# First token tile's experts looked up in two halves of the heads, its row gathers begun during the key rounds, and the key compares fed from PSUM

## The chip, the cores and the metric

The program runs on 1 core of one Trainium2 chip, alone, as one launch. The metric is the device time of one execution in microseconds (us). The core has TensorE (PE; its weight loads are listed as PEld), VectorE (DVE), ScalarE (ACT), GpSimd (POOL), SyncE (SP, which here only issues transfers) and 16 DMA engines. Each engine runs its own instruction list in order.

## The reference, cut to what matters

The program computes two layers of a first block (feed-forward, three attentions, feed-forward), a recurrent mixer, and at the end a layer of 16,384 experts ("peer") and a last normalization. Only the peer layer is touched. For 512 tokens of width 1024:

```
qry    = (t @ w_q).reshape(n_tok, 8 heads, 2 sides, 128)
scores = einsum("thpd,hpkd->thpk", qry, sub_keys)              # 128 keys a side
s_top, i_top = top_k(scores, 16)
cand     = (s_top[:, :, 0, :, None] + s_top[:, :, 1, None, :])   # 16 x 16 pairs a head
cand_idx = (i_top[:, :, 0, :, None] * 128 + i_top[:, :, 1, None, :])
best, pos = top_k(cand, 16)
idx  = take_along_axis(cand_idx, pos);  gate = softmax(best)
act  = gelu(einsum("td,thkd->thk", t, u_tab[idx]))
out  = einsum("thk,thkd->td", gate * act, v_tab[idx])
```

So each token uses 8 x 16 = 128 of the 16,384 experts; an expert is one row of `u_tab` and one row of `v_tab`, 1024 numbers each.

## The kernel before

The peer layer works on four token tiles of 128 tokens. Tile 0 takes the rows of its own experts from HBM ("gathered"). Tiles 1 to 3 (384 tokens) do it densely: all 16,384 experts are computed for all 384 tokens, and a gate matrix that is zero nearly everywhere multiplies them. The layer has four stages.

**Key rounds** (`topk`, L1600 to L1624). Sixteen rounds j, two for a head. A round multiplies a weight column block by the hidden state, scores it against the keys (L1607), and VectorE takes the 16 best of each of four tiles (`top16`). At odd j GpSimd adds the candidate sums `cand` (L1618) and VectorE takes the best pairs of tiles 0 and 1 (`pair`). A weight block is loaded into `raw`, rounded by ScalarE into `wh` (L91), and the rest `wl` is subtracted (L92): in this stage by GpSimd. From j = 4 on each round also computes one dense group of 128 experts in advance (`ahead`, 53 of the 128 groups in all, list `EARLY`) and stores it to HBM.

**Lookup** (`found`). It turns positions of best pairs into key numbers and gates: a wide compare on VectorE (L1674), a product on GpSimd (L1675), a sum on VectorE (L1678), twice. For tile 0 it ends in `eidx` and `egate`. For tiles 1 to 3, TensorE turns the results into a PSUM bank `pt` (L1706) and ScalarE copies them to SBUF tiles `sel`. Before the change the lookups of tile 0 and tile 1 run together after the last key round, with five `ahead` groups beside them (L1658).

**Scatter** (`scatter`, L1712 to L1751). It builds the gate matrix of tiles 1 to 3 in 24 blocks of 16 tokens. For every token a one-hot `lt` (VectorE, L1728) and a weighted one-hot `rt` are made and multiplied on TensorE into `g`; `rt` is made partly by ScalarE (L1734, L1735), partly by a VectorE compare (L1737) and a GpSimd product (L1738). A block holds two half blocks of eight tokens. The other `ahead` groups run here, 36 in number, and so do the lookups of tiles 2 and 3.

**Dense stage** (`dense`, L1552 to L1577). 16 groups g of eight expert groups e; from e = 1 of the next group on, eight `down` blocks use the eight results. The gates `gt` of a group are loaded at e = 0, 1.5 MB in one transfer. The product is split as `eh` (ScalarE) and `el` (GpSimd, L1569).

**The gathered rows of tile 0** (`gathered`) are a generator of 256 rows of each token, four from `pur` then four from `pvr` in turn. One step (`more(1)`) issues the gather of one row on GpSimd (L1472, 512 KB) and uses an earlier one on VectorE: a dot product with `ht` (L1479) or a multiply-add into `acc` (L1486). LOOK says how many steps lie between a row's issue and its use. Four buffers `er` hold rows, so a gather waits until the row four before it is used. `more` is called at chosen places of the scatter and the dense stage; issues and uses keep their order among themselves, and a list scheduler puts them between the other instructions.

PSUM has three `bk` banks for linear products, two `sc`, two `g` and one `pt`.

Of the kernel before, what the change touches and what calls it, by code (L numbers as in the profile page):

```python
# [9 lines left out]
F = mybir.dt.float32  # L10
FR = mybir.dt.float32r
BF = mybir.dt.bfloat16
I32 = mybir.dt.int32
# [13 lines left out]
D = 1024  # L27
# [23 lines left out]
class K:  # L51
# [1403 lines left out]
    def gathered(self, ht):  # L1455
# [4 lines left out]
        NB, LOOK = 4, 2  # L1460
# [7 lines left out]
        for n in range(len(steps) + LOOK):  # L1468
            if n < len(steps):
                table, s = steps[n]  # L1470
                r = rows[n] = mp.tile([128, D], F, name="er", tag="er", bufs=LOOK + 2)
                order(nc.gpsimd.indirect_dma_start(r, None, a[table], bass.IndirectOffsetOnAxis(ap=self.eidx[:, s:s + 1], axis=0)))  # L1472
            if n >= LOOK:
                table, s = steps[n - LOOK]
                r, b, i = rows.pop(n - LOOK), s // NB, s % NB
                if table == "pur":
# [4 lines left out]
                    if i == NB - 1:  # L1481
                        w = ws[b] = mp.tile([128, NB], F, name="ew", bufs=3)
                        nc.scalar.activation(w, dots.pop(b), AF.Gelu)
                        nc.vector.tensor_mul(w, w, self.egate[:, NB * b:NB * b + NB])
# [4 lines left out]
    def peer(self):  # L1489
# [6 lines left out]
        with tc.tile_pool(name="peer", bufs=1) as mp:  # L1496
# [3 lines left out]
            sel = [mp.tile([128, DW], F, name=f"sel{i}") for i in range(4)]  # L1500
            ht = self.by_token(rc)
            self.eidx = mp.tile([128, 128], I32, name="eidx")
            self.egate = mp.tile([128, 128], F, name="egate")
# [23 lines left out]
    def dense(self, ep, mp, gd, ad, dn, expert, more):  # L1527
# [24 lines left out]
        for g in range(16):  # L1552
            wh, wl = [], []
            for e in range(8):
# [17 lines left out]
                more(0 if j in EARLY else 1 + (e == 0))  # L1572
# [6 lines left out]
    def topk(self, sp, hh, hl, io, sel, gd, ahead, more):  # L1579
# [13 lines left out]
        with tc.tile_pool(name="topk1", bufs=1) as mp:  # L1593
# [31 lines left out]
            first = mp.tile([128, 4, 8, 16], F, name="first")  # L1625
            nc.vector.tensor_copy(first, si[:, :, :, 0])
            nc.vector.tensor_copy(second, si[:, :, :, 1])

            sf = first.rearrange("p t h k -> p (t h) k")
            pk = mp.tile([128, 32, 16], F, name="pk")  # L1630
            rw = row.rearrange("p t h k -> p (t h) k")
            nc.vector.tensor_tensor(pk, sf, io[:, 160:176].unsqueeze(1).to_broadcast([128, 32, 16]), op=OP.add)
            nc.vector.tensor_copy(rw[:, :, 0:1], pk[:, :, 0:1])
            nc.vector.tensor_tensor(rw[:, :, 1:16], pk[:, :, 1:16], pk[:, :, 0:15], op=OP.subtract)
        with tc.tile_pool(name="topk2", bufs=1) as mp:
# [22 lines left out]
            run(pairs(0), pairs(1), fill(5, 0))  # L1658
# [3 lines left out]
    def found(self, mp, t, best, pos, second, row, io, sel):  # L1662

        nc = self.nc
        b3, b4 = [128, 8, 16], [128, 4, 16, 16]
# [5 lines left out]
        def look(dst, src, table, values, op):  # L1671
            for q in (slice(0, 4), slice(4, 8)):
# [12 lines left out]
        z = mp.tile([128, 8], F, name="gz", bufs=2)  # L1685
# [12 lines left out]
        if t * 128 < SPT:  # L1698
            nc.vector.scalar_tensor_tensor(res[0], res[0], 128.0, res[1], op0=OP.mult, op1=OP.add)
            nc.vector.tensor_copy(self.eidx, res[0].rearrange("p h k -> p (h k)"))  # L1700
# [6 lines left out]
        for i in range(3):  # L1707
            nc.scalar.copy(sel[i][:, s0:s0 + 128], pt[:, i * 128:i * 128 + 128])
# [215 lines left out]
```

## Time and profile before

| | us |
|---|---|
| median of 3 runs | 4782.38 (4781.05 to 4784.15) |
| profiled execution, its time | 4788.46 |
| its span | 4786.7 |
| key rounds, 16 of them | about 3316 to 3459 |
| from the last key scores to the first full scatter block | 3459 to 3516 |
| scatter | 3516 to 3840 |
| dense stage with its last products | 3840 to 4740 |
| end | 4740 to 4787 |

Over the span PE is busy 94%, DVE 66%, ACT 40% and POOL 26%. These shares say little, since the stages have different limits: the peer layer has to be read stage by stage, in the table of busy times by stretch, and in the list of who waited for whom in a stretch. All times below are counted from the start of the span.

### The profile page before, as it was taken

What the parts mean: (1) busy time and instruction counts of PE and PEld (TensorE: products, weight loads), DVE (VectorE), ACT (ScalarE), POOL (GpSimd) and SP (SyncE); (2) the same over time, 40 slices, a digit from 0 to 9 for tenths busy, and PEclk for the clock granted to TensorE, in tenths of its full rate; (3) what the DMA queues carried; (4) which work ended last, traced back from release to release, by engine and by line L of the source; (5) the groups of instructions that cost most, each with busy time, mean ns of one, the idle gap of its engine ahead of it and who ended that gap; (6) DMA issues with size and microseconds to landing.
All of it is one profiled execution on the core that took longest, in us unless ns stands there. A gap on an engine that the chain in (4) does not pass through costs nothing. (4 is left out here: it accounts for less than half of the span.)

```text
span 4786.7 us, 63161 instructions
## 1 busy us (share of the span) xinstructions
PE 4504.0 (94%) x23078; PEld 3895.2 (81%) x23078; DVE 3179.3 (66%) x5824; ACT 1919.9 (40%) x3465; POOL 1223.6 (26%) x1053
## 2 busy tenths in 40 slices
PE   9999998999999999989999998988968889999998
PEld 7887876788888888767788777876967889999998
DVE  4447878754454458787644467876598767777776
ACT  3225665632232246646422333223355633333333
POOL 0001112210000011121300101223577744555543
PEclk9999999999999999999999999998988999999999
DMA  3234323433323344233423334123346787788884
GB/s 128 95 105 131 98 83 93 151 113 97 97 93 97 97 126 112 87 98 98 158 96 97 122 90 141 45 65 119 119 168 217 256 270 272 272 282 284 296 279 171
DMA packets 282359, 696.58 MB, mean 146 GB/s; under 512 B 32864, under 2 KB 98304, under 8 KB 278976
## 3 DMA queue, kind: packets, MB, share of 16 engines
q1 hardware_dynamic: 245184, 558.30, 36.5%
q0 software_dynamic: 36864, 134.23, 8.0%
q8 instruction: 183, 3.00, 0.3%
q14 instruction: 128, 1.05, 0.1%
HBM read 597.18 MB, written 72.17 MB: 140 GB/s over the span
## 5 line engine op out<-in xcount | busy, mean ns | idle before, releaser
L91 ACT CAST wh<-raw 128x1024 fp32r<-128x1024 f32 (+3 forms) x773 | 765.9, 993 | 1669.1 <-PE bk L113 959.4
L113 PE MATMUL bk<-hh,wh 128*128 128x512 f32 (+1 forms) x3016 | 1140.3, 378 | 15.8 <-ACT hh L237 9.0
L113 PE MATMUL bk<-hh,wl 128*128 128x512 f32 (+1 forms) x3016 | 1133.8, 376 | 8.2 <-DVE wl L92 8.2
L113 PE MATMUL bk<-hl,wh 128*128 128x512 f32 (+1 forms) x3016 | 1133.2, 376 | 0.5 <-DVE hl L238 0.5
L92 DVE TENSOR_TENSOR wl<-raw,wh 128x1024 fp32r<-128x1024 f32 (+3 forms) x664 | 812.2, 1224 | 174.5 <-ACT wh L91 166.9
L113 PEld LDWEIGHTS bk<-hh,wh 128*128 128x128 f32 x3016 | 574.6, 191 | 97.0 <-ACT hh L237 9.4
L113 PEld LDWEIGHTS bk<-hh,wl 128*128 128x128 f32 x3016 | 573.9, 190 | 87.5 <-DVE wl L92 9.3
L113 PEld LDWEIGHTS bk<-hl,wh 128*128 128x128 f32 x3016 | 574.8, 191 | 79.1 <-issue 2.2
L203 POOL TENSOR_TENSOR sq<-sq,sqt 128x512 f32<-128x512 f32 x61 | 102.2, 1675 | 1199.7 <-ACT sqt L199 1180.9
L92 POOL TENSOR_TENSOR wl<-raw,wh 128x1024 fp32r<-128x1024 f32 (+2 forms) x109 | 258.3, 2371 | 583.3 <-ACT wh L91 463.7
L113 PE MATMUL bk<-eh,wl 128*128 128x384 f32 x1024 | 354.8, 346 | 41.7 <-DVE wl L92 41.4
L113 PE MATMUL bk<-eh,wh 128*128 128x384 f32 x1024 | 350.7, 342 | 2.5 <-ACT act L1513 1.8
L113 PE MATMUL bk<-el,wh 128*128 128x384 f32 x1024 | 350.1, 342 | 0.6 <-POOL el L1569 0.6
L113 PE MATMUL bk<-gh,wh 128*128 128x512 f32 x704 | 273.9, 389 | 0.0
L113 PE MATMUL bk<-gh,wl 128*128 128x512 f32 x704 | 273.9, 389 | 0.0
L113 PE MATMUL bk<-gl,wh 128*128 128x512 f32 x704 | 273.9, 389 | 0.0
L1569 POOL TENSOR_TENSOR el<-act,eh 128x384 fp32r<-128x384 f32 x128 | 176.4, 1382 | 336.5 <-ACT eh L1568 327.2
L276 DVE TENSOR_TENSOR t<-bk,rr 128x512 f32<-128x512 f32 x88 | 60.8, 691 | 269.1 <-PE bk L113 269.1
L113 PEld LDWEIGHTS bk<-eh,wl 128*128 128x128 f32 x1024 | 194.9, 190 | 53.4 <-DVE wl L92 53.4
L1486 DVE SCALAR_TENSOR_TENSOR acc<-er,ew,acc 128x1024 f32<-128x1024 f32 x128 | 179.7, 1404 | 80.3 <-DMA er<-in_pvr,eidx 80.3
L1479 DVE CUSTOM_DVE_ANT_0 er<-er,ht 128x1024 f32<-128x1024 f32 x128 | 172.8, 1351 | 77.9 <-DMA er<-in_pur,eidx 77.9
L285 DVE SCALAR_TENSOR_TENSOR x<-bk,x 128x512 f32<-128x512 f32 x96 | 66.4, 692 | 231.4 <-PE bk L113 231.4
(709 smaller groups left out, 8784.5 us busy)
## 6 DMA issues: line engine op xcount, KB each, us to landing
raw<-in_wi SPq DMA_DIRECT2D x176, 512.0 KB, 3.6
raw<-in_pu SPq DMA_DIRECT2D x128, 512.0 KB, 4.7
raw<-in_pv SPq DMA_DIRECT2D x128, 512.0 KB, 4.3
raw<-in_wo SPq DMA_DIRECT2D x64, 448.0 KB, 3.3
raw<-in_mg SPq DMA_DIRECT2D x48, 512.0 KB, 3.7
gate_d<-stage SPq DMA_DIRECT2D x24, 1024.0 KB, 7.0
gt<-gate_d SPq DMA_DIRECT2D x16, 1536.0 KB, 11.0
raw<-in_wo SPq DMA_DIRECT2D x32, 512.0 KB, 3.5
```

The lines of the kernel that those rows point to most:

```text
L91: self.nc.scalar.copy(wh[:, :n], raw[:, :n])
L92: (eng or self.nc.vector).tensor_sub(wl[:, :n], raw[:, :n], wh[:, :n].bitcast(F))
L113: self.nc.tensor.matmul(ps, x[:, c], y[k], start=(n == 0), stop=(n == 3 * kk - 1))
L203: nc.gpsimd.tensor_add(self.sq, self.sq, t)
L276: nc.vector.tensor_mul(t2, pb, rr)
L285: nc.vector.scalar_tensor_tensor(self.x[m], ps, 0.5, self.x[m], op0=OP.mult, op1=OP.add)
L1479: order(nc.vector.tensor_tensor_reduce(out=r, in0=r, in1=ht, scale=1.0, scalar=0.0, op0=OP.mult, op1=OP.add, accum_out=dots[b][:, i:i + 1]))
L1486: order(nc.vector.scalar_tensor_tensor(acc, r, ws[b][:, i:i + 1], acc, op0=OP.mult, op1=OP.add))
L1569: nc.gpsimd.tensor_sub(q, act, h.bitcast(F))
```

## The change

Four things are edited.

1. Tile 0's lookup runs in two halves of four heads, inside the key rounds, at the end of j = 7 and of j = 15; `eidx` and `egate` become two tiles of 64 columns. The preparation of `row` and `second` is halved with it.
2. Row steps of tile 0 start earlier: three in each of rounds 8 to 15, two with each of the five `ahead` groups after the last round. In return the dense stage has them only at e = 0, 1 and 7 and in the `down` blocks. Over all 34 steps come before the scatter (none before), 48 in it (48 before), and the dense stage has 176 (211 before). LOOK goes from 2 to 3, the buffers stay four.
3. The scatter's compares L1728 and L1737 read the selected keys from the PSUM bank (now an `sc` bank, one for each tile in turn) and not from SBUF; the copy of `sel[0]` goes.
4. In every second scatter block one `ahead` group's `wl` moves from GpSimd to VectorE, 12 in all.

```diff
-        NB, LOOK = 4, 2
+        NB, LOOK = 4, 3
...
-                r = rows[n] = mp.tile([128, D], F, name="er", tag="er", bufs=LOOK + 2)
-                order(nc.gpsimd.indirect_dma_start(r, None, a[table], bass.IndirectOffsetOnAxis(ap=self.eidx[:, s:s + 1], axis=0)))
+                r = rows[n] = mp.tile([128, D], F, name="er", tag="er", bufs=LOOK + 1)
+                order(nc.gpsimd.indirect_dma_start(r, None, a[table], bass.IndirectOffsetOnAxis(ap=self.eidx[s // 64][:, s % 64:s % 64 + 1], axis=0)))
...
-                more(0 if j in EARLY else 1 + (e == 0))
+                more((2 - g % 2 if e == 0 else 1) if e in (0, 1, 7) else 0)
...
+                if j % 8 == 7:
+                    hs = slice(j // 8 * 4, j // 8 * 4 + 4)
...
+                    for _ in self.found(mp, 0, best[:, 0, hs], pos[:, 0, hs], second[:, 0, hs], row[:, 0, hs], io, sel, j // 8):
+                        pass
+                if j >= 8:
+                    more(3)
...
-            run(pairs(0), pairs(1), fill(5, 0))
+            run(pairs(1), fill(5, 2))
...
-        pt = self.bank("pt")
+        pt = self.bank("sc")
...
-                nc.vector.tensor_tensor(lt, keys(8), wide(sel[0], 0, 8), op=OP.is_equal)
+                nc.vector.tensor_tensor(lt, keys(8), wide(pt, 0, 8, i - s0), op=OP.is_equal)
...
-                    nc.vector.tensor_tensor(r, keys(4 - n), wide(sel[1], u + n, u + 4), op=OP.is_equal)
-                    nc.gpsimd.tensor_tensor(r, r, wide(sel[2], u + n, u + 4), op=OP.mult)
+                    nc.vector.tensor_tensor(r, keys(4 - n), wide(pt, u + n, u + 4, i - s0 + 128), op=OP.is_equal)
+                    nc.gpsimd.tensor_tensor(r, r, wide(sel[1], u + n, u + 4, i), op=OP.mult)
...
-                    ahead(1, nc.gpsimd if tb % 2 else None)
+                    ahead(1)
```

The order of instructions on POOL changes at three places. First, POOL in the key rounds, from the candidate sums of round 11 to those of round 13 (`cand` are candidate sums, `wl` weight splits, `er` the gathers). Before:

```order
L1618 TENSOR_TENSOR cand<-sv 128x4x8
L92 TENSOR_TENSOR wl<-raw,wh 128x1024
L1618 TENSOR_TENSOR cand<-sv 128x4x16
L92 TENSOR_TENSOR wl<-raw,wh 128x1024 x3
L1618 TENSOR_TENSOR cand<-sv 128x4x8
```

After:

```order
L1619 TENSOR_TENSOR cand<-sv 128x4x8
L92 TENSOR_TENSOR wl<-raw,wh 128x1024
L1619 TENSOR_TENSOR cand<-sv 128x4x16
L1472 DMA er<-in_pvr,eidx_29050 128x1024 x2
L1472 DMA er<-in_pur,eidx_29050 128x1024
L92 TENSOR_TENSOR wl<-raw,wh 128x1024 x2
L1472 DMA er<-in_pur,eidx_29050 128x1024 x3
L92 TENSOR_TENSOR wl<-raw,wh 128x1024
L1619 TENSOR_TENSOR cand<-sv 128x4x8
```

Six gathers now stand in two rounds among four weight splits; 21 stand between the candidate sums of round 7 and those of round 15.

Second, POOL from the last candidate sum to the first product of the scatter (`eq` are the lookup's products). Before:

```order
L92 TENSOR_TENSOR wl<-raw,wh 128x1024
L1675 TENSOR_TENSOR eq<-eq,row 128x1024 x2
L92 TENSOR_TENSOR wl<-raw,wh 128x1024
L1675 TENSOR_TENSOR eq<-eq,row 128x1024 x2
L1675 TENSOR_TENSOR eq<-eq,second 128x1024 x4
L1472 DMA er<-in_pur,eidx 128x1024
L92 TENSOR_TENSOR wl<-raw,wh 128x1024
L1738 TENSOR_TENSOR rt<-rt,sel_29020 128x384
```

After:

```order
L1682 TENSOR_TENSOR eq<-eq,row 128x1024
L92 TENSOR_TENSOR wl<-raw,wh 128x1024 x2
L1682 TENSOR_TENSOR eq<-eq,second 128x1024
L1472 DMA er<-in_pur,eidx_29050 128x1024 x3
L1472 DMA er<-in_pvr,eidx_29050 128x1024
L1682 TENSOR_TENSOR eq<-eq,row 128x1024 x2
L1472 DMA er<-in_pvr,eidx_29050 128x1024 x3
L1472 DMA er<-in_pur,eidx_29050 128x1024
L1682 TENSOR_TENSOR eq<-eq,second 128x1024 x2
L1472 DMA er<-in_pur,eidx_29050 128x1024 x3
L1472 DMA er<-in_pvr,eidx_29050 128x1024 x2
L1747 TENSOR_TENSOR rt<-rt,sel_29019 128x384
```

Eight products, three splits and one gather become six products, two splits and thirteen gathers.

Third, POOL in the dense stage, around the change from group 8 to group 9 (`el` is made once for each e). Before, from e = 6 and 7 of group 8 on:

```order
L1569 TENSOR_TENSOR el<-act,eh 128x384 x2
L1472 DMA er<-in_pvr,eidx 128x1024
L1569 TENSOR_TENSOR el<-act,eh 128x384
L1472 DMA er<-in_pvr,eidx 128x1024
L1472 DMA er<-in_pur,eidx 128x1024
L1569 TENSOR_TENSOR el<-act,eh 128x384
L1472 DMA er<-in_pur,eidx 128x1024 x3
L1472 DMA er<-in_pvr,eidx 128x1024
```

After, from e = 3 to 7 of group 8 on:

```order
L1570 TENSOR_TENSOR el<-act,eh 128x384 x5
L1472 DMA er<-in_pvr,eidx_29051 128x1024
L1570 TENSOR_TENSOR el<-act,eh 128x384
L1472 DMA er<-in_pvr,eidx_29051 128x1024
L1570 TENSOR_TENSOR el<-act,eh 128x384
L1472 DMA er<-in_pvr,eidx_29051 128x1024
L1472 DMA er<-in_pur,eidx_29051 128x1024 x2
L1570 TENSOR_TENSOR el<-act,eh 128x384
L1472 DMA er<-in_pur,eidx_29051 128x1024 x2
L1472 DMA er<-in_pvr,eidx_29051 128x1024 x4
```

The rows used at e = 7, 0 and 1 are now those issued three steps earlier, in the `down` blocks, ahead of the five `el`; a gather that stands behind the `el` of e = 7 is used in the first `down` block.

## Rows read from the trace of the kernel before

**Rows 1.** Stretches: length, busy us (x) of PE, PEld, DVE, ACT, POOL; PEclk; DMA, GB/s.

```profile
3373.00:3459.00 86.00, 86.00 (x453) 76.81 (x452) 51.31 (x348) 28.48 (x40) 44.03 (x45) 1.00 0.38 117
3459.00:3516.00 57.00, 32.10 (x170) 30.27 (x170) 45.90 (x98) 15.63 (x29) 37.95 (x23) 0.76 0.25 86
3516.00:3840.00 324.00, 270.05 (x1624) 261.04 (x1623) 272.85 (x358) 204.91 (x468) 236.40 (x160) 0.89 0.68 233
3840.00:4740.00 900.00, 847.31 (x4709) 833.65 (x4708) 682.41 (x788) 298.19 (x427) 450.13 (x336) 0.98 0.81 276
```

**Rows 2.** PE's waits, 3459 to 3516: us in total, times, longest.

```profile
PE pt L1706 <- DVE res L1695: 14.0, 1, 14.0
```

**Rows 3.** PE's waits, 3516 to 3840.

```profile
PE g L1742 <- POOL rt L1738: 42.4, 25, 4.3
```

**Rows 4.** Waits of PE, then of DVE, 3840 to 4740.

```profile
PE bk L113 <- DVE wl L92: 46.6, 29, 5.1
...
DVE acc L1486 <- DMA er<-in_pvr,eidx: 79.2, 23, 9.7
DVE er L1479 <- DMA er<-in_pur,eidx: 57.4, 23, 7.9
```

**Rows 5.** Groups in 3373 to 3459: count | busy us, mean ns | idle before.

```profile
L92 POOL TENSOR_TENSOR wl<-raw,wh 128x1024 fp32r<-128x1024 f32 x17 | 40.5, 2385 | 31.7 <-ACT wh L91 31.7
```

**Rows 6.** Tile `er`, all instructions: ns min/median/max; idle us, times; landing from issue.

```profile
L1472 POOL DMA_INDIRECT er<-in_pur,eidx x128: 933/1263/1978, 3506.8 to 4694.3; - x128
L1479 DVE CUSTOM_DVE_ANT_0 er<-er,ht x128: 1207/1218/3417, 3520.8 to 4698.8; 128x1024 f32<-128x1024 f32 x128
...
  issue: 28.0, 123
...
DMA to landing us min/median/max: 4.1/6.9/12.7
```

**Rows 7.** Group of the lookup's products on POOL in 3459 to 3516.

```profile
L1675 POOL TENSOR_TENSOR eq<-eq,row 128x1024 f32<-128x1024 f32 x4 | 11.3, 2834 | 3.2 <-DVE eq L1674 3.2
```

**Rows 8.** Groups of the scatter's compares, products and splits in 3516 to 3840.

```profile
L1728 DVE TENSOR_TENSOR lt<-io,sel 128x1024 f32<-128x1024 f32 x46 | 71.3, 1549 | 1.1 <-PE g L1742 1.1
L1738 POOL TENSOR_TENSOR rt<-rt,sel 128x256 f32<-128x256 f32 x47 | 69.2, 1472 | 33.4 <-DVE rt L1737 31.0 <-ACT stage L1744 2.3
L1737 DVE TENSOR_TENSOR rt<-io,sel 128x256 f32<-128x256 f32 x47 | 36.5, 776 | 4.5 <-PE g L1742 3.8 <-ACT rt L1735 0.7
L1737 DVE TENSOR_TENSOR rt<-io,sel 128x384 f32<-128x384 f32 x47 | 33.3, 708 | 0.0
L92 POOL TENSOR_TENSOR wl<-raw,wh 128x1024 fp32r<-128x1024 f32 x11 | 29.8, 2713 | 1.7 <-ACT wh L91 1.7
```

**Rows 9.** Single lines, whole span: ns min/median/max, first and last start.

```profile
L1543 DVE TENSOR_TENSOR x<-bk,x x128: 544/552/559, 3891.1 to 4768.8; 128x384 f32<-128x384 f32 x128
L1565 DVE TENSOR_TENSOR act<-act,gt x128: 544/670/1377, 3851.6 to 4735.8; 128x384 f32<-128x384 f32 x128
L1728 DVE TENSOR_TENSOR lt<-io,sel x48: 1209/1622/3411, 3511.3 to 3825.8; 128x1024 f32<-128x1024 f32 x48
L1737 DVE TENSOR_TENSOR rt<-io,sel x96: 405/546/2726, 3512.5 to 3827.9; 128x384 f32<-128x384 f32 x48, 128x256 f32<-128x256 f32 x48
L1738 POOL TENSOR_TENSOR rt<-rt,sel x96: 612/1420/3465, 3513.2 to 3828.9; 128x384 f32<-128x384 f32 x48, 128x256 f32<-128x256 f32 x48
```

**Rows 10.** Timelines around 4340 to 4355, of SP, POOL, DVE and PE: start, duration.

```profile
4340.40 0.53 SPq L1558 DMA_DIRECT2D gt<-gate_d  x1
...
4342.59 1.76 POOL L1472 DMA_INDIRECT er<-in_pvr,eidx  x1
...
4352.13 1.28 DVE L1486 SCALAR_TENSOR_TENSOR acc<-er,ew,acc 128x1024 f32<-128x1024 f32 x1 [6.94 <-DMA er<-in_pvr,eidx]
4353.33 1.22 DVE L92 TENSOR_TENSOR wl<-raw,wh 128x1024 fp32r<-128x1024 f32 x1
...
4354.60 0.44 PE L113 MATMUL bk<-eh,wl 128*128 128x384 f32 x1 [1.30 <-DVE wl L92]
```

More of the change, by code (lines that the diff above doesn't have):

```diff
@@ L1499, in peer @@
             nc.sync.dma_start(io, a["iota"])
-            sel = [mp.tile([128, DW], F, name=f"sel{i}") for i in range(4)]
+            sel = [mp.tile([128, DW], F, name=f"sel{i}") for i in range(3)]
+            self.found_t = {}
             ht = self.by_token(rc)
-            self.eidx = mp.tile([128, 128], I32, name="eidx")
-            self.egate = mp.tile([128, 128], F, name="egate")
+            self.eidx = [mp.tile([128, 64], I32, name=f"eidx{i}") for i in range(2)]
+            self.egate = [mp.tile([128, 64], F, name=f"egate{i}") for i in range(2)]
             rows = self.gathered(ht)
@@ L1624, in topk @@
                     ahead(1, nc.gpsimd)
[L1625 to L1634, printed above, removed]
+                if j % 8 == 7:
+                    hs = slice(j // 8 * 4, j // 8 * 4 + 4)
+                    b4 = [128, 4, 4, 16]
+                    nc.vector.tensor_copy(second[:, :, hs], si[:, :, hs, 1])
+                    pk = mp.tile(b4, F, name="pk")
+                    nc.vector.tensor_copy(pk, si[:, :, hs, 0])
+                    nc.vector.tensor_tensor(pk, pk, io[:, 160:176].unsqueeze(1).unsqueeze(1).to_broadcast(b4), op=OP.add)
+                    rw = row[:, :, hs]
+                    nc.vector.tensor_copy(rw[:, :, :, 0:1], pk[:, :, :, 0:1])
+                    nc.vector.tensor_tensor(rw[:, :, :, 1:16], pk[:, :, :, 1:16], pk[:, :, :, 0:15], op=OP.subtract)
+                    for _ in self.found(mp, 0, best[:, 0, hs], pos[:, 0, hs], second[:, 0, hs], row[:, 0, hs], io, sel, j // 8):
+                        pass
+                if j >= 8:
+                    more(3)
         with tc.tile_pool(name="topk2", bufs=1) as mp:
@@ L1656, in fill, with found @@
                     yield
-            run(pairs(0), pairs(1), fill(5, 0))
+            run(pairs(1), fill(5, 2))
             for t in range(1, 4):
                 run(self.scatter(mp, t, io, sel, gd, ahead, more), *[pairs(t + 1)] if t < 3 else [])
-    def found(self, mp, t, best, pos, second, row, io, sel):
+    def found(self, mp, t, best, pos, second, row, io, sel, half=None):
         nc = self.nc
-        b3, b4 = [128, 8, 16], [128, 4, 16, 16]
+        nh = 8 if half is None else 4
+        b3, b4 = [128, nh, 16], [128, 4, 16, 16]
         res = [mp.tile(b3, F, name=f"res{i}", bufs=2) for i in range(3)]
```

28 lines of the change are left out of this document (15 added, 13 removed).

## Prediction

> **What bounds the kernel now.** I read the table of busy times by stretch first. [...] From the last key scores to the scatter PE works 32 of 57 us, in the scatter 270 of 324, in the dense stage 847 of 900 [rows 1]. [...] The lists of waits say who ends the idle time. Before the scatter it is the lookup of tile 1, whose result must pass TensorE (14.0 us in one piece) [rows 2]. In the scatter it is GpSimd's product `rt`, 42.4 us in 25 waits [rows 3]. In the dense stage it is VectorE's split `wl`, 46.6 us in 29 waits, and VectorE itself stood 79.2 + 57.4 us waiting for gathered rows [rows 4].
>
> The timeline shows one such wait whole [rows 10]. At 4340.40 SP issues the 1.5 MB load of `gt`. At 4342.59 GpSimd issues a gather; it has stood behind an `el` in GpSimd's list. It lands at 4352.1, over 9 us later where 6.9 us is the median [rows 6]. VectorE stands 6.94 us for it with `wl` behind it in its list, and PE waits 1.30 us for that `wl`. This comes back at nearly every change of group.
>
> **Dense stage.** The change leaves the number of `down` steps alone and takes 35 steps out of the e loop. What decides is the order: the rows used at e = 7, 0 and 1 are now issued during the `down` blocks, before the `gt` load, and those behind the `el` of e = 7 are used only in the first `down` block. Between issue and use lie three steps, in the e loop each a whole linear product or more, against a landing of 6.9 us, at worst 12.7 [rows 6]. Both kernels have four buffers, so no row can be issued before the row four earlier is used; what is won is that it does not stand behind an `el`. I take away 32 of the 46.6 us and 10 of the 18 us of clock: **-42**. Bounds: -15, if another wait (ScalarE's rounding, the transfers) ends a little later at the same places, and all of it, -64. A group's 56 us (900/16) have room for eleven or twelve steps of 1.22 us [rows 6], so no new wait on VectorE is visible.
>
> **Scatter.** Now the compares. Where VectorE's second input lies in PSUM its time hardly varies: L1543 takes 544 to 559 ns over 128 instructions, while L1565, the same size with both inputs in SBUF, takes 544 to 1377 [rows 9]. The compares are of the second kind today. `lt` takes 1549 ns in the mean and 1209 at least, the 256-wide `rt` 776 and 405, the 384-wide 708, for which I take L1543's 552 [rows 8, 9]. Of each there are 48: 16.3 + 17.8 + 7.5 = 41.6 us less on VectorE. Twelve splits come to it, 12 x 1.22 = 14.6 us [rows 10]. VectorE falls from 272.9 to 246. On GpSimd the twelve splits at 2.71 go, 32.5 us, and the 256-wide products, which take 1472 ns and 612 at least, may give 48 x 0.86 = 41 us: 236 falls to about 162 [rows 1, 8, 9]. The number of row steps is 48 in both. A floor is PE's own work at full clock, 324 - 54 - 36 = 234 us. VectorE's floor is 246 us and its 51 us of idle time, some of which is waiting for rows and goes: 272 to 297. That is -27 to -52. I take 20 of the 42.4 us of waits for `rt` and 14 of the 36 us of clock, **-34**. The upper bound is -10, for a scatter that stays tied to VectorE's order.
>
> [...]
>
> **Key rounds.** Here the change can only cost. A round takes 86/8 = 10.75 us. Rounds 8 to 15 get 21 gathers on GpSimd, each 1.26 us and 0.23 us (28.0/123) to the next [rows 6], 31.3 us; and two products of the first half lookup, 5.7 us [rows 7]: 37.0 us. GpSimd idles 86 - 44.0 = 42.0 us there. VectorE gets 21 steps x 1.22 = 25.6 us, and compares and sums of the half lookup, four of 1.2 us and some 3 us of small ones: 33 us, into 86 - 51.3 = 34.7 us of idle time. Both just fit, and nothing is left over. GpSimd has the weight splits that feed PE (17 x 2.39) behind the gathers in its list [rows 5], and a gather waits there for its buffer. Splits have three buffers, so some lateness is covered. I take **+6**, bounds 0 and +59 (below, the serial case).
>
> **Before the scatter.** GpSimd had eight products of 2.83, three splits of 2.39 and a gather of 1.49, 31.3 us; it gets six, two and thirteen, 41.1 us [rows 5 to 7]. That is +10 on the engine that ends the lookup and starts `rt`. The stretch has 19 us in which GpSimd idles, and VectorE has two compares and two sums fewer, so the lower bound is -5. Thirteen rows through four buffers, each landing in 6.9 us and used in 1.22, need 13/4 x 8.1 = 26 us, which is the upper bound. **+10**.
>
> The halving of `pk`, `row` and `second` moves as much work as it leaves, and three fewer 128-wide copies on ScalarE are off the path: 0.
>
> **The sum**: -42 - 34 + 6 + 10 = -60, against the profiled execution's 4788.5: 4728.5. The median of the runs is 6.1 lower, so I forecast **4722**.
>
> **Rivals.**
> - All goes well: the scatter reaches VectorE's lower figure (-52), the dense stage gives -50, rounds and gap cost 5: about -97, 4685. For it: PE's floor in the scatter is lower still. Against: two engines are full in the rounds.
> - The stall at the change of group only moves: -15 in the dense stage, the rest as priced, 4749. For it: four buffers as before. Against: the order on GpSimd.
> - Products and two-input steps exclude each other. L1565 against L1543 shows such steps stretching beside GpSimd [rows 9]. In a round GpSimd has 44.0/8 = 5.5 us of work, 4.5 us of gathers, and would stand 3 x 1.22 us for steps: 13.7 us instead of 10.75, +23 instead of +6 over eight rounds: 4739. [...]
> - **Slower**: the rounds run in series. GpSimd waits in its list for a buffer that VectorE has not freed, VectorE waits for the row to land, and the splits wait behind both. A round is then 5.5 + 4.5 + 6.9 + 1.22 = 18.1 us, +59 over eight; the gap costs its 26; the scatter gives 27, the dense stage 42: +16, 4798. It decides from about 16 us a round. Against: a row used in a round was issued in the round before, 10 us earlier, and the median landing is 6.9.
> - That row steps bring nothing by being moved, as VectorE does them anyway, is the second rival at its end, -15.
>
> **Chances**: forecast 0.52, all well 0.13, moved stall 0.14, exclusion 0.12, serial 0.09. About 0.2%, 9.6 us, is what a measurement of this kernel can tell from no change. The forecast, its better form, the exclusion and the moved stall lie beyond that but for their tails: faster 0.85; the tails and a serial case of smaller price: same 0.07; slower 0.08. The range runs from the case where all goes well to past the moved stall, 4685 to 4765.
>
> **What would show it.** Dense: PE's waits for `wl` from 46.6 to about 15 us, VectorE's waits for rows from 137 to under 40, clock 0.99. Scatter: L1728's successor at 1.2 us in nearly all cases, the 256-wide product near 0.7, about 290 us long, clock above 0.9. Rounds: PE gaps at `wl` from round 9 on, a few us together; if they reach 40 us the serial rival is right. Gap: scatter's first blocks about 15 us later than now. The forecast is wrong if the scatter starts over 40 us later, or if the 29 waits stay in the dense stage.

## The result

The changed kernel takes **4706.2 us** (median of four runs, 4702.6 to 4707.9) against 4782.0 us of the kernel before beside it: a ratio of 0.984, 95% interval 0.9823 to 0.9857. The forecast was 4722 us, the range 4685 to 4765. The profiled execution of the changed kernel took 4702.6 us, its span 4700.8, against 4788.5 and 4786.7 before. So the profiled executions differ by 85.9 us, the medians by 75.7: the profiled execution before was slower than the four runs beside it, the one of the changed kernel was the fastest of its four. The stages below are cut from these two executions, so their differences come to some 10 us more than the medians show, and it is not known in which stage.

A first view cuts the span where the work changes, as [rows 1] do, but at the changed kernel's own places: key rounds, the stretch before the scatter, the scatter, the dense stage with its end. Columns as in [rows 1].

```profile
3373.00:3474.00 101.00, 89.79 (x453) 79.70 (x452) 83.52 (x398) 31.68 (x46) 71.40 (x67) 0.96 0.61 198
3474.00:3544.00 70.00, 41.53 (x206) 39.11 (x205) 58.89 (x134) 23.63 (x44) 54.28 (x37) 0.73 0.54 177
3544.00:3810.00 266.00, 242.09 (x1560) 235.84 (x1561) 244.93 (x351) 196.47 (x452) 188.57 (x147) 0.96 0.81 278
3810.00:4700.00 890.00, 867.96 (x4916) 862.88 (x4914) 639.91 (x773) 314.51 (x443) 435.31 (x308) 0.99 0.77 265
```

PE, which never paused in the key rounds before, now stands 11 of 101 us there; GpSimd and VectorE work 71 and 84 us of them, where they had 44 and 51 of 86. Then come longer gains: in the scatter PE's clock rises from 0.89 to 0.96, in the dense stage PE stands 22 of 890 us, at 0.99.

For comparing kernels I cut at instructions, not at round numbers: the first score matmul of the key rounds, the score matmul of the last round, the first and the last store of `gate_d`, the end of the span. All kernels of this study by those marks (one profiled execution each; the last columns are medians and the ratio to the kernel before on the same chip):

| kernel | key rounds | before the scatter | scatter | dense | median | ratio, 95% interval |
|---|---|---|---|---|---|---|
| before | 140.8 | 63.2 | 313.6 | 951.5 | 4782.0 | |
| changed | 155.6 | 71.3 | 265.3 | 891.0 | 4706.2 | 0.984 (0.9823–0.9857) |
| e1_gelu | 152.4 | 75.2 | 266.0 | 895.0 | 4707.7 | 0.9823 (0.981–0.9837) |
| e2_look2 | 155.7 | 81.0 | 279.0 | 913.0 | 4744.7 | 0.99 (0.9885–0.9915) |
| e3_sbuf | 155.3 | 73.4 | 286.2 | 894.0 | 4728.7 | 0.9867 (0.9852–0.9882) |
| e4_wlpool | 155.6 | 73.1 | 274.1 | 892.8 | 4719.9 | 0.9845 (0.983–0.986) |
| e5_densepl | 155.3 | 71.6 | 263.8 | 920.7 | 4735.6 | 0.9894 (0.9879–0.9909) |
| e6_bpsum | 140.6 | 63.3 | 284.4 | 954.7 | 4759.4 | 0.9941 (0.9925–0.9956) |
| e7_norounds | 142.9 | 54.7 | 253.3 | 928.3 | 4693.5 | 0.9811 (0.9795–0.9828) |
| e8_fill0 | 155.2 | 60.3 | 267.3 | 900.7 | 4705.2 | 0.9824 (0.9805–0.9842) |
| e9_one | 144.5 | 56.8 | 264.0 | 920.9 | 4707.9 | 0.9835 (0.9805–0.9865) |
| e10_down | 144.5 | 53.5 | 253.7 | 901.4 | 4671.1 | 0.9761 (0.9734–0.9789) |
| e11_mix | 144.4 | 56.8 | 263.1 | 902.7 | 4686.8 | 0.9793 (0.9765–0.9821) |
| e12_eloop | 144.5 | 53.5 | 254.0 | 940.6 | 4713.9 | 0.9846 (0.9817–0.9875) |

The kernel before ran 4786 to 4791 us on the chips of the experiments, so medians of different rows are compared by their ratios. How far one stage can be trusted is seen where kernels share its code: the dense stage of changed, e3 and e4 took 891.0, 894.0 and 892.8, their key rounds 155.6, 155.3 and 155.6. Under 4 us I read nothing into a stage.

The span before the first mark is code that no kernel here changes; it took 3312.0 (e7) to 3324.2 us (e9), so that medians differ by some us that no edit made.

So the change itself reads: key rounds +14.8, before the scatter +8.1, scatter -48.3, dense stage -60.5; together -85.9. For the last two, the kernel before between the same marks:

```profile
3521.60:3835.20 313.60, 259.65 (x1556) 251.07 (x1556) 267.01 (x347) 198.04 (x454) 231.71 (x156) 0.89 0.69 236
3835.20:4786.70 951.50, 885.43 (x4918) 870.03 (x4916) 700.90 (x827) 312.81 (x447) 460.25 (x342) 0.98 0.78 266
```

The changed kernel's PE is busy 241.6 and 868.1 us between these marks, in 1558 and 4916 matrix products. So of the scatter's 48.3 us 30.3 are PE's idle time and 18.0 its busy time, shorter at a granted clock of 0.95 for 0.89; of the dense stage's 60.5 us 43.2 and 17.3, at 0.99 for 0.98.

PE's waits in the four stretches (us in total, times, longest), then VectorE's waits for rows in the dense stage, all of the changed kernel:

```profile
PE sc L1608 <- ACT qt L1604: 9.7, 4, 3.6
PE bk L113 <- POOL wl L92: 1.5, 1, 1.5
...
PE sc L1713 <- DVE ew L1484: 8.7, 1, 8.7
PE sc L1713 <- DVE res L1685: 8.4, 1, 8.4
PE g L1751 <- DVE lt L1737: 7.2, 1, 7.2
...
PE g L1751 <- POOL rt L1747: 11.6, 4, 5.2
PE g L1751 <- DVE lt L1737: 9.9, 2, 5.5
...
PE bk L113 <- DVE wl L92: 4.7, 5, 1.2
...
DVE acc L1486 <- DMA er<-in_pvr,eidx: 19.5, 7, 5.7
DVE er L1479 <- DMA er<-in_pur,eidx: 12.1, 6, 4.7
```

The 42.4 us of [rows 3] have become 11.6; of [rows 4], PE's 46.6 us have become 4.7 and VectorE's 136.6 us of waiting for rows 31.6. The first two lines are new; the larger is a wait for ScalarE's copy `qt`, of which the prediction said nothing. VectorE has a new wait of its own in the dense stage, 41.8 us for the loads of columns computed early (`act_d`), where it was 0.5 us before; little of it reaches PE.

### The profile page after: what moved, and what is told of

Same layout as the page of the kernel before. It is cut to its first block, busy times and chain, and to the rows that moved or that the text cites. A ratio compares the mean times of both kernels' runs of the same rounds, so it can differ in the third digit from the quotient of the medians.

```text
span 4700.8 us, 63144 instructions
## 1 busy us (share of the span) xinstructions
PE 4476.2 (95%) x23078; PEld 3878.3 (83%) x23078; DVE 3134.8 (67%) x5853; ACT 1925.9 (41%) x3467; POOL 1192.0 (25%) x1041
## 5 line engine op out<-in xcount | busy, mean ns | idle before, releaser
L92 DVE TENSOR_TENSOR wl<-raw,wh 128x1024 fp32r<-128x1024 f32 (+3 forms) x676 | 834.1, 1235 | 194.1 <-ACT wh L91 187.1
L92 POOL TENSOR_TENSOR wl<-raw,wh 128x1024 fp32r<-128x1024 f32 (+2 forms) x97 | 222.5, 2297 | 550.4 <-ACT wh L91 420.1
L1472 POOL DMA_INDIRECT er<-in_pvr,eidx x128 | 188.2, 1471 | 120.9 <-DVE dot L1479 67.8
L1570 POOL TENSOR_TENSOR el<-act,eh 128x384 fp32r<-128x384 f32 x128 | 159.9, 1259 | 224.1 <-ACT eh L1569 213.8
L1472 POOL DMA_INDIRECT er<-in_pur,eidx x128 | 183.8, 1436 | 105.4 <-DVE acc L1486 67.7
```

The costliest lines, as they stand in the source:

```text
L92: (eng or self.nc.vector).tensor_sub(wl[:, :n], raw[:, :n], wh[:, :n].bitcast(F))
L1570: nc.gpsimd.tensor_sub(q, act, h.bitcast(F))
```

## The experiments

### What the scatter's gain is made of

Four kernels take one thing out of the changed kernel, or put one into the kernel before. The first has the compares read the keys from SBUF again:

```diff
+        nc.scalar.copy(sel[3][:, s0:s0 + 128], pt[:, 0:128])
...
-  nc.vector.tensor_tensor(lt, keys(8), wide(pt, 0, 8, i - s0), op=OP.is_equal)
+  nc.vector.tensor_tensor(lt, keys(8), wide(sel[3], 0, 8, i), op=OP.is_equal)
...
-  nc.vector.tensor_tensor(r, keys(4 - n), wide(pt, u + n, u + 4, i - s0 + 128), op=OP.is_equal)
+  nc.vector.tensor_tensor(r, keys(4 - n), wide(sel[0], u + n, u + 4, i), op=OP.is_equal)
```

> The changed kernel with the compares of the scatter reading the keys from SBUF again (one copy of 128 columns more per tile on ScalarE); GpSimd stays without the twelve splits. Theory C (the compares' source made the scatter shorter): lt goes from 1206 back to about 1550 ns and the 256-wide rt from 408 to about 750, VectorE gets about 35 us more work in the scatter, and its length goes from 265 to 290 us or more, the whole to about 4730. Theory W (GpSimd without the twelve splits made it shorter): lt and rt are slower, but the scatter stays under 275 us and the whole under 4716, since VectorE's extra time is covered.

Measured: scatter 286.2 us, ratio 0.9867. Theory C holds in its direction, at a smaller size: the scatter falls short of the 290 us, `lt` takes 1434 and the 256-wide `rt` 541 ns for the 1550 and 750 expected, and VectorE works 22.7 us more between the marks (267.1 against 244.4), not 35. The groups of compares and products in the scatter, first of the changed kernel, then of this one (count | busy us, mean ns | idle before):

```profile
L1747 POOL TENSOR_TENSOR rt<-rt,sel 128x256 f32<-128x256 f32 x46 | 63.2, 1374 | 15.6 <-DVE rt L1746 13.3 <-ACT stage L1753 2.3
L1747 POOL TENSOR_TENSOR rt<-rt,sel 128x384 f32<-128x384 f32 x46 | 45.7, 993 | 49.5 <-DVE rt L1746 35.7 <-PE bk L113 10.8 <-DVE pf L1676 2.0
L1737 DVE TENSOR_TENSOR lt<-io,sc 128x1024 f32<-128x1024 f32 x45 | 54.3, 1206 | 0.0
L1746 DVE TENSOR_TENSOR rt<-io,sc 128x384 f32<-128x384 f32 x46 | 24.9, 541 | 0.0
L1746 DVE TENSOR_TENSOR rt<-io,sc 128x256 f32<-128x256 f32 x46 | 18.8, 408 | 0.4 <-ACT wh L91 0.2 <-ACT act L1514 0.2
```

```profile
L1748 POOL TENSOR_TENSOR rt<-rt,sel 128x256 f32<-128x256 f32 x46 | 58.6, 1274 | 25.8 <-DVE rt L1747 18.4 <-ACT rt L1744 5.8 <-ACT rt L1745 1.6
L1748 POOL TENSOR_TENSOR rt<-rt,sel 128x384 f32<-128x384 f32 x46 | 56.6, 1230 | 42.1 <-DVE rt L1747 27.4 <-ACT rt L1744 11.2 <-DVE pa L1699 1.2
L1738 DVE TENSOR_TENSOR lt<-io,sel 128x1024 f32<-128x1024 f32 x45 | 64.5, 1434 | 0.0
L1747 DVE TENSOR_TENSOR rt<-io,sel 128x384 f32<-128x384 f32 x45 | 31.8, 707 | 0.0
L1747 DVE TENSOR_TENSOR rt<-io,sel 128x256 f32<-128x256 f32 x45 | 24.3, 541 | 2.2 <-PE g L1752 1.8 <-ACT wh L91 0.4
```

From PSUM the compares lie, in the mean, at about the least that they took from SBUF in the kernel before (1209 and 405 ns for two of them, [rows 9]); from SBUF they are 228, 166 and 133 ns longer.

GpSimd gains too, though its 256-wide product alone does not show it (1374 ns beside PSUM compares, 1274 beside SBUF compares). The 384-wide product goes the other way, 993 against 1230 ns, and over the scatter GpSimd works 188.2 us in the changed kernel, 205.9 in this one. The durations have two levels, and what VectorE runs meanwhile goes with the level. Two cases in the changed kernel: the 256-wide product beside a compare from PSUM, then beside a weight split, which reads two operands from SBUF:

```profile
3665.39 1.21 DVE L1737 TENSOR_TENSOR lt<-io,sc 128x1024 f32<-128x1024 f32 x1
3665.55 0.62 POOL L1747 TENSOR_TENSOR rt<-rt,sel 128x256 f32<-128x256 f32 x1 [1.50 <-DVE rt L1746]
...
3618.72 1.88 DVE L92 TENSOR_TENSOR wl<-raw,wh 128x1024 fp32r<-128x1024 f32 x1
3619.48 1.59 POOL L1747 TENSOR_TENSOR rt<-rt,sel 128x256 f32<-128x256 f32 x1
```

Counted over all 48 of the 256-wide products of the changed kernel: seven overlap compares but no split and no row step, and all seven take 612 to 618 ns. Forty overlap a split or a row step (a dot product or multiply-add), and 38 of these take over 1.4 us. In the kernel before, where the compares read SBUF, 15 overlap compares but no split and no row step, and 13 of those 15 take over 0.9 us, eleven of them 1.46 to 1.60. So the compares did stretch the products, and from PSUM they do not; but few products meet compares alone.

The second puts the twelve splits back on GpSimd:

```diff
-                    ahead(1)
+                    ahead(1, nc.gpsimd if tb % 2 else None)
```

> The changed kernel with the twelve splits wl of the odd blocks of the scatter back on GpSimd; the compares still read PSUM. Theory C (the compares' source made the scatter shorter): VectorE gains the 12 x 1.56 us of splits back, GpSimd has room (it works 192 of 275 us), the scatter stays within 8 us of 265 and the whole within 8 us of 4706. Theory W (the splits' leaving GpSimd made it shorter): GpSimd gets 12 x 2.7 = 32 us, PE's waits for rt from GpSimd go from 12.0 back to 30 us or more, the scatter goes to 285 us or more and the whole to about 4725.

Measured: scatter 274.1 us, just past theory C's 8 us; PE's waits for GpSimd's `rt` 31.5 us in 15 waits, as theory W had it. In this kernel 24 more matrix products, one dense group, stand ahead of the first store; with the stretch before it the two are 10.6 us longer than in the changed kernel. The splits are worth some 9 to 11 us there; in the whole, 0.9845 against 0.984, they can't be told from nothing.

The third has two steps between a row's issue and its use, with the same four buffers:

```diff
-        NB, LOOK = 4, 3
+        NB, LOOK = 4, 2
...
-  r = rows[n] = mp.tile([128, D], F, name="er", tag="er", bufs=LOOK + 1)
+  r = rows[n] = mp.tile([128, D], F, name="er", tag="er", bufs=LOOK + 2)
```

> The changed kernel with rows used two steps behind their issue again, with the same four buffers; the places of the steps stay as changed. Theory L (the three steps between issue and use made the dense stage shorter): VectorE's waits for rows go from 32 us back to 100 or more there, PE's waits for wl from 4.7 to over 25 us, the dense stage from 890.9 to about 930 us and the whole to about 4740. Theory P (the places of the steps in a group of columns made it shorter, the gathers going ahead of the el): the dense stage is within 10 us of 890.9 and the whole at most 4718.

Measured: dense 913.0 us, between the two theories, and, expected by neither, the scatter 279.0 and the stretch before it 81.0. Whole 4744.7, ratio 0.99. The waits in its dense stage are halfway back too:

```profile
PE bk L113 <- DVE wl L92: 20.2, 18, 2.5
...
DVE acc L1486 <- DMA er<-in_pvr,eidx: 47.8, 15, 7.1
DVE er L1479 <- DMA er<-in_pur,eidx: 43.0, 14, 8.2
```

So the third step works in three stages: 22 us in the dense stage, 14 in the scatter, 10 before it.

The fourth is the kernel before with the PSUM compares alone (the edit is the reverse of the first, with the bank `sc` kept until the tile's scatter ends).

> The kernel before with the compares of the scatter alone reading the keys from PSUM (one copy less per tile on ScalarE); all else as before, so the lookup is whole, nothing begins in the key rounds, two steps lie between a row's issue and its use, and twelve splits wl stay on GpSimd. Theory A (parts add up): taking it out of the changed kernel lengthened the scatter by 21 us, so putting it in alone shortens it from 313.6 to about 293, the whole by about 20, a ratio of 0.996. Theory G (GpSimd's load decides while its splits and two-step rows stay): lt goes to 1.21 us and rt to 0.41, but PE's waits for rt from GpSimd stay near 42 us, the scatter over 305 us and the ratio over 0.998.

Measured: scatter 284.4 us, ratio 0.9941. `lt` 1211 ns, and PE's waits for GpSimd's `rt` fall from 42.4 to 28.4 us though GpSimd keeps its splits. GpSimd works 200.8 us between the marks, 231.7 before, in 155 and 156 instructions: this is the clearest sign that PSUM compares free GpSimd as well. Theory A's direction holds, its size (293 us, 0.996) was too small; put in alone the edit brings 29 us, taken out last it cost 21, so the parts overlap.

### Where the key rounds' 14.8 us come from

In the changed kernel's rounds ScalarE's list shows this (timeline of ScalarE, then of PE: start, duration, idle time before and what ended it):

```profile
3411.65 0.49 ACT L1514 ACTIVATE act<-bk 128x384 f32<-128x384 f32 x1
3421.50 0.21 ACT L1483 ACTIVATE ew<-dot 128x4 f32<-128x4 f32 x1 [9.36 <-DVE dot L1479]
3421.61 1.03 ACT L91 CAST wh<-raw 128x1024 fp32r<-128x1024 f32 x1
3422.54 0.58 ACT L1604 COPY qt<-bk 128x512 f32<-128x512 f32 x1
...
3423.17 1.22 PE L1608 MATMUL sc<-keys,qt 128*128 128x128 f32 x4 [3.58 <-ACT qt L1604]
```

A 0.2 us Gelu stands 9.4 us for VectorE's last dot of a batch, and the next round's `wh` and `qt` stand behind it. One kernel moves the Gelu behind the next round's copies:

```diff
-  w = ws[b] = mp.tile([128, NB], F, name="ew", bufs=3)
-  nc.scalar.activation(w, dots.pop(b), AF.Gelu)
+  late.append((n + (3 if b < 3 else 0), b, ...))   # emitted three row steps later,
+  # and for b < 3 pinned behind what stands in ScalarE's list by then
```

> The changed kernel with one thing moved: in the rounds over the keys the Gelu of a batch of dots is put on ScalarE behind the next round's copies of qt and sc instead of ahead of them (the first three batches alone). Theory S (ScalarE's list held the rounds up): in the changed kernel ScalarE stood 9.4, 1.4 and 6.7 us for a dot with the next round's wh and qt behind it, and the key rounds ended 14.9 us later than before; with the Gelu behind, the rounds that took 16.2, 15.1 and 13.5 us take 10.7 to 11.5, the last key matmul comes 10 to 13 us earlier (3460 to 3463 us) and the whole is 8 to 13 us shorter, some 4695 us. Theory F (VectorE and GpSimd are simply full in the rounds): VectorE works 82.7 of the 100.3 us from 3373 on, so the wait turns up at another place (sc's two buffers, or wl); the last key matmul stays within 4 us of 3473 and the whole within 4 us of 4706.

Measured: last key matmul at 3472.6, whole 4707.7, ratio 0.9823 (its interval overlaps the changed kernel's). The key rounds began 2.6 us later here, so between the marks they are 3.2 us shorter, less than one stage can tell. The two rounds behind the moved Gelu take 12.5 and 10.6 us instead of 16.2 and 15.2, as theory S says, but the three behind them take 11.9, 13.5 and 14.5 instead of 10.7, 10.7 and 13.5. PE's waits in this kernel's rounds:

```profile
PE bk L113 <- POOL wl L92: 6.8, 3, 2.7
PE sc L1613 <- ACT qt L1609: 3.1, 2, 2.1
```

The wait went to the splits behind GpSimd's gathers. Theory F is nearer: of 12.8 us that the last five rounds were over 10.7 each, 9.5 stay. The next kernels remove the row steps there. The first has none in the rounds and none before the scatter, and the old places in the dense stage:

```diff
-                if j >= 8:
-                    more(3)
...
-            run(pairs(1), fill(5, 2))
+            run(pairs(1), fill(5, 0))
...
-   more((2 - g % 2 if e == 0 else 1) if e in (0, 1, 7) else 0)
+   more(0 if j in EARLY else 1 + (e == 0))
```

> The changed kernel without row steps in the key rounds and in the stretch before the scatter, with the dense stage's steps at their old places; the half lookup of tile 0, three steps ahead, the PSUM compares and the splits on VectorE stay. Theory R (the row steps cost the 14.9 us of the key rounds and the longer gap): a round takes 10.7 us again, but for the one with the first half lookup (12.9), so the key rounds end 10 to 13 us earlier than in the changed kernel, and the first store of the scatter comes at about 3525 us instead of 3545. Theory H (the half lookups cost it, by their compares and products): the rounds stay within 4 us and the first store comes no earlier than 3538. By either the dense stage gets the 34 steps back and is longer than 891 us.

Measured: key rounds 142.9, first store at 3509.6, scatter 253.3, dense 928.3, ratio 0.9811. Theory R holds and falls short: without the early row steps the three stages ahead of the dense one are 12.7, 16.6 and 12.0 us shorter than in the changed kernel, 41.3 together. So the four stages take 1379.2 us against the changed kernel's 1383.2 although the dense stage has its old order; the intervals of the two ratios overlap, so the wholes are not told apart. What is left of the half lookup by itself, against the kernel before: 2.1 us more in the rounds, the round with the first half takes 12.9 us instead of 10.7 in every kernel that has it, and 8.5 us less before the scatter.

The second takes only the ten steps before the scatter out:

```diff
-            run(pairs(1), fill(5, 2))
+            run(pairs(1), fill(5, 0))
...
-   more((2 - g % 2 if e == 0 else 1) if e in (0, 1, 7) else 0)
+   more(2 if e == 0 else e in (1, 7) or (e == 3 and g % 8 == 4))
```

> The changed kernel with the ten row steps between the key rounds and the scatter taken out there and put into the e loop of the dense stage (two at e = 0 of every group, and two more steps in all). In the changed kernel VectorE does twelve dots and sums of rows of 1.2 to 3.4 us, about 22 us, among the compares and sums of tile 1's lookup, and PE stands 8.7 and 8.4 us for that lookup and 7.2 for the first lt. Theory V (these steps are on the path to the scatter): the stretch from the last key matmul to the first store goes from 71.3 to 55 to 62 us, the scatter stays within 5 us of 265, the dense stage within 4 of 891; the whole comes to about 4695, 0.981 to 0.982 of the kernel before. Theory T (the ten steps cost as much wherever they are done, since VectorE or GpSimd is the bound): what the stretch gains the scatter or the dense stage loses, and the whole stays within 4 us of the changed kernel.

Measured: before the scatter 60.3 us, scatter 267.3, dense 900.7, ratio 0.9824. Both theories in part: the steps were on the way to the scatter (11.0 us), and in the e loop they cost 9.7 us, so nearly nothing is left, and the whole is what theory T expected.

### What a row step's place in the dense stage is worth

First the changed kernel with the old places in the dense stage alone (the last two lines of the diff of e7_norounds).

> The changed kernel with the row steps of the dense stage at their old places (one at every e, two at e = 0, none where the columns were computed early, one in each down block); three steps ahead and four buffers as changed. The run with two steps ahead had 913 us in the dense stage, against 890.9 in the changed kernel and 951.5 in the kernel before. Theory P (places make most of it, 38 of 60.6 us): the dense stage goes to 925 us or more, with PE's waits for wl at 30 us or more; the whole is 4740 or more. Theory L (with three steps ahead the places matter little): dense stage under 905 us, the whole under 4722.

Measured: dense 920.7 us, PE's waits for `wl` 23.8 us in 14 waits, ratio 0.9894. Theory P in its direction, each number short of its bound: the places are worth 30 us. Compared with e7_norounds (928.3, the same places), the 34 steps moved out of the dense stage save it 7.6 us.

Then four kernels without steps between the key rounds and the scatter, which differ in where the freed steps go.

> The changed kernel with one row step in each of the rounds 8 to 15 in place of three, none in the stretch before the scatter, and the 26 steps that this frees in the dense stage's e loop (two at e = 0, one at 1, 3 and 7). Without any row step there the key rounds took 142.9 us, the stretch after them 54.7 and the scatter 253.3, against 155.6, 71.3 and 265.3 in the changed kernel. Theory Q (up to a step or so a round is free, since VectorE and GpSimd each have 17 of 100 us left with three): key rounds under 145 us, stretch under 58, scatter 253 to 265; the dense stage, at about 1 us for each step moved to it as in the run with ten, some 912 to 917 us; the whole about 4683, a ratio of 0.979. Theory N (any row step in a round lengthens it): key rounds 148 or more, the whole at 4695 or more.

> No row steps in the key rounds nor before the scatter; in the dense stage two at e = 0, one at e = 1 and 7, and 26 of the freed steps as second ones in the down blocks (two of eight in each). Theory P (the place in the group decides): a step in a down block is issued before the next load of gt and costs less than the 1 us of one in the e loop, so the dense stage is 900 to 910 us, with the key rounds at 143, the stretch at 55, the scatter at 253: the whole 4665 to 4675, a ratio of 0.975 to 0.977. Theory V (each step costs VectorE's time wherever it is): dense stage 920 us or more, the whole 4690 or more.

> One row step in each of the rounds 8 to 15, none before the scatter; in the dense stage two at e = 0, one at e = 1 and 7, and one more in each down block's fifth product, three more in the first groups. Theories Q and P together: key rounds under 145, stretch under 58, scatter 253 to 265, dense stage 895 to 905; the whole 4665 to 4675, a ratio of 0.975 to 0.977. Theory N or V: as with the two runs beside it, 4690 or more.

> No row steps in the key rounds nor before the scatter, as in the run beside it, but the freed 26 steps in the e loop (one at e = 3 in every group, one at e = 5 in ten) in place of the down blocks. Theory P: those steps stand behind the load of gt and the el, the dense stage is 10 us or more longer than with the steps in the down blocks, 915 to 928 us; the whole 4680 to 4693. Theory V: both dense stages agree within 5 us.

Their edits in the dense stage (e9 and e11 have `more(1)` in rounds 8 to 15, e10 and e12 none):

```diff
 e9   more(2 if e == 0 else e in (1, 3, 7))
 e10  more(2 if e == 0 else e in (1, 7));     in down: more(0 if last else 2 if m in (1, 5) and g < 13 else 1)
 e11  more(2 if e == 0 else e in (1, 7) or (e == 3 and g < 3));   in down: more(0 if last else 2 if m == 4 else 1)
 e12  more(2 if e == 0 else e in (1, 3, 7) or (e == 5 and g < 10))
```

e10_down gives 4671.1 us, a ratio of 0.9761 (0.9734 to 0.9789): both within what theory P expected. It has the lowest median here; its four stages take 1353.1 us, 30 less than the changed kernel's. e12_eloop has the same 26 steps in the e loop and gives 0.9846; up to the dense stage the two are alike within 0.3 us, then 901.4 against 940.6 us. Theory P holds, and more strongly than priced (e12 lies past its 928 and 4693 us): 1.5 us for each of the 26. One step a round costs the rounds nothing that one stage can tell (144.5 with it in e9; 144.5 and 142.9 without, in e10 and e7), but lengthens the scatter to 264.0 and 263.1 us where it is 253.7 and 254.0 without. So e9 and e11 miss theory Q's totals (4707.9 for about 4683, 4686.8 for at most 4675), e9 also by its e loop, whose dense stage took 920.9 us for at most 917; e11 keeps each stage's range, with the scatter near its upper end. Stretches of e10 (dense stage), then of e12, and their waits of PE and of VectorE for rows:

```profile
3773.00:4673.00 900.00, 870.08 (x4916) 862.94 (x4914) 682.06 (x829) 311.81 (x447) 476.65 (x342) 0.99 0.80 282
...
PE bk L113 <- DVE wl L92: 14.7, 14, 2.1
...
DVE acc L1486 <- DMA er<-in_pvr,eidx: 29.4, 13, 5.0
DVE er L1479 <- DMA er<-in_pur,eidx: 19.9, 10, 4.6
```

```profile
3774.00:4714.00 940.00, 888.38 (x4917) 877.35 (x4915) 699.20 (x829) 312.62 (x447) 485.97 (x342) 0.97 0.78 270
...
PE bk L113 <- DVE wl L92: 29.6, 17, 3.2
PE bk L113 <- ACT eh L1569: 6.9, 8, 1.9
...
DVE er L1479 <- DMA er<-in_pur,eidx: 42.6, 13, 7.4
DVE acc L1486 <- DMA er<-in_pvr,eidx: 36.8, 12, 5.4
```

One change of group in e12 shows how it happens (timelines of SP, GpSimd, VectorE, ScalarE and PE):

```profile
4156.78 0.53 SPq L1559 DMA_DIRECT2D gt<-gate_d  x1
...
4157.38 1.39 POOL L1570 TENSOR_TENSOR el<-act,eh 128x384 fp32r<-128x384 f32 x1 [1.04 <-ACT eh L1569]
4158.93 1.76 POOL L1472 DMA_INDIRECT er<-in_pvr,eidx  x1 [0.16 <-issue]
...
4170.13 1.29 DVE L1486 SCALAR_TENSOR_TENSOR acc<-er,ew,acc 128x1024 f32<-128x1024 f32 x1 [4.97 <-DMA er<-in_pvr,eidx]
4173.25 0.56 DVE L1566 TENSOR_TENSOR act<-act,gt 128x384 f32<-128x384 f32 x1 [1.83 <-DMA act<-act_d]
4174.19 1.27 DVE L1486 SCALAR_TENSOR_TENSOR acc<-er,ew,acc 128x1024 f32<-128x1024 f32 x1
4175.38 1.22 DVE L92 TENSOR_TENSOR wl<-raw,wh 128x1024 fp32r<-128x1024 f32 x1
...
4173.84 0.51 ACT L1569 CAST eh<-act 128x384 fp32r<-128x384 f32 x1 [7.18 <-DVE act L1566]
...
4174.42 0.41 PE L113 MATMUL bk<-eh,wh 128*128 128x384 f32 x1 [0.78 <-ACT eh L1569]
4176.66 0.69 PE L113 MATMUL bk<-eh,wl 128*128 128x384 f32 x1 [1.65 <-DVE wl L92]
```

It is the picture of [rows 10]: a gather goes out behind the load of `gt` and an `el`, at 4158.93, and lands at 4170.04. VectorE stands 4.97 us for it, then 1.83 us for the load of an `act` computed early; another row step follows, and `act`, `eh` and `wl` reach PE late, twice.

The two traces also tell how often this happens. Of the 208 gathers of the dense stage, 41 in e10 and 59 in e12 are under way together with a load of `gt`. These land after 9.1 and 9.3 us in the median, the others after 6.7 and 6.2. That the load itself makes them late, and not something else at the change of group, no run isolates.

## Why the prediction was right or wrong

**Dense stage, -42 forecast, -60.5 measured, within the bounds.** The mechanism is the one named: the order of gathers against the `gt` load, and the third step. Both parts of the term were too small. I took away 32 of the 46.6 us of waits; 41.9 went, and PE's idle time fell by 43.2 us. I took 10 us for the clock; PE's busy time for the same products fell by 17.3. The clock terms here and in the scatter, 18 and 36 us, are what 900 us at 0.98 and 324 us at 0.89 lack of 1.00 [rows 1]. The clock record of the kernel before has two levels, 1.00 and 0.50: from 3490 to 3510 us, where PE works 3.1 of 20 us, it is 0.50 throughout. No run isolates what the clock alone is worth. Taking parts out singly gives 22 us for the third step and 30 for the places, and 8 for the steps that left (e2, e5, e5 against e7); they come to 60, though single parts need not add up. Expected waits for `wl` of about 15 us came to 4.7, those for rows of under 40 to 31.6, the clock of 0.99 as said.

**Scatter, -34 forecast, -48.3 measured, within the bounds.** The compares came out as worked: they fell to 1206, 408 and 541 ns. The twelve splits did not: all splits on VectorE take 1564 ns in the mean there, so that its busy time, 267.0 us between the marks, fell by 22.7 us where I had 27; that 245 stands beside an expected 246 is partly luck, since the 246 was for the longer stretch of [rows 1]. GpSimd's part was mis-sized: the 256-wide product was to fall from 1472 towards 700 ns and is 1374, so GpSimd works 189 us, not 162. That the compares stretch the product was right; the wrong step was to free all 48 products. In the kernel before only 15 of them overlap compares and neither a split nor a row step; in the changed kernel 40 overlap one of those, which still read two operands from SBUF. The gain was yet larger than forecast, 30.3 us of idle time for 20, and 18.0 us of busy time for the 14 of the clock. The third step between issue and use brings 14 us in this stage (e2), which I had priced at nothing because the number of steps is the same. The forecast of about 290 us was for the 324 us of [rows 1]; between the marks it would be 280, and 265 were measured. Reading PSUM cost the compares nothing that shows: the 128x1024 one took 1161 to 1217 ns from PSUM, 1209 at least from SBUF.

**Key rounds, +6 forecast, +14.8 measured, within the bounds.** The cause is the one priced, the row steps: without them (e7) the rounds take 142.9 us. VectorE's load came as worked, 83.5 us for 51.3 + 33; GpSimd's was lighter, 71.4 us, 27 more than before and not 37. The place was wrong: I put the wait at the splits behind GpSimd's gathers; the trace shows it first in ScalarE's list, of which the prediction said nothing, where the Gelu on a batch of dots has the next copies behind it. e1 removes that wait and gets 3.2 us back, less than a stage can tell; then PE waits for the splits, 6.8 us. So ScalarE's list was where lateness became visible, and the load is the cause. The serial rival (16 us a round) shows in one round of eight.

**Before the scatter, +10 forecast, +8.1 measured.** Right in sum, and that by luck, from two terms I had not separated: the half lookup takes 8.5 us away (e7), the row steps add 16.6, since VectorE does them among the compares and sums of tile 1's lookup. I priced GpSimd; PE's waits there are for VectorE (8.7, 8.4 and 7.2 us).

**The sum and the rivals.** All stages went the way forecast; the gains were short by 32.8 us, the costs by 6.9. The moved stall fell (4.7 us of waits for `wl` left), and so did the serial rounds. The rival of engines that exclude each other came out below its +23, but it is not refuted: twelve dots in the key rounds take 1432 ns in the mean where [rows 6] have 1218 as the median, and in the kernel before L1565 takes 545 to 557 ns in the 35 cases in which GpSimd does nothing beside it, 1367 ns in the median of the 66 that overlap GpSimd's arithmetic. How much of the 14.8 us it makes no run separates. The case where all goes well stood at 4685; its gains were exceeded in the dense stage, its cost of 5 us in the rounds and gap was not kept.

**What I did not see.** I counted the 34 early steps as a gain of the dense stage. They save it 7.6 us at the old places and some 10 at good ones (901.4 of e10 against 891.0), and cost 41.3 us ahead of it. Begun early, the rows are a loss of about 30 us inside a change that gains by its other parts.

**Open.** Why the scatter is 253 to 254 us where no row step precedes it (e7, e10, e12) and 263 to 267 where one does. VectorE works 232 us in the one and 244 (changed) or 241 (e9) in the other. The number of steps is not the reason: between the marks VectorE uses 45 rows in e10 and 45 in e11. The same instructions take longer: in e9 the splits take 1492 ns in the mean, 1300 in e10; in e11 10 of the 48 256-wide products overlap compares and neither a split nor a row step, 19 in e10. So the row steps fall at other places beside GpSimd's work; why these places cost more was not isolated.

## What to carry to other kernels

Steps that are moved into an earlier stage "because engines idle there" must be priced against what they leave: here 34 steps cost 41 us ahead and had cost 8 to 10 where they were, while the place of the same steps within a loop was worth 39 us (e10 against e12). Before filling idle time on two engines, read the in-order list of the third that waits for them: here a 0.2 us instruction stood 9.4 us for a late result, and the next round's two copies stood behind it. Moving that one instruction is no cure where the load itself is too much: here the wait only moved (e1). Give prefetched transfers as long a lead as the buffers allow, here three steps with four buffers; one step more with the same buffers was worth 36 us in two stages.

## What the runs showed of the hardware

With one input in PSUM the compare `lt` took 1161 to 1217 ns in all 48 cases of the changed kernel, 1205 to 1215 in the 24 of them that overlap GpSimd's arithmetic; with both in SBUF it took 1209 to 3411 in the kernel before [rows 9]. GpSimd's time was shorter as well: its 256-wide product took 612 to 618 ns in all seven cases in which it met PSUM compares and neither a split nor a row step (changed kernel), 606 to 661 in all 13 of e6, and over 0.9 us in 13 of 15 beside compares from SBUF (kernel before). Beside VectorE's splits and row steps, which have both operands in SBUF, 38 of 40 took over 1.4 us in the changed kernel. Whoever moves one operand to PSUM to free GpSimd has to ask how much of GpSimd's work meets that instruction at all.

Gathers of 512 KB that were under way together with the 1.5 MB load of `gt` landed later: in the dense stage of the kernel before 58 of 208, after 8.6 us in the median against 6.7 for the others; in the changed one 40 of 174, after 9.1 against 6.2.
